# An encoder block on one core: the loads of the down projection issued as two halves each

## The chip, the cores and the metric

The kernel runs on one core of a Trainium2 chip. The metric is the device time of one execution in microseconds (us); the kernel before has a median of 2466.58 us over three runs.

## The reference, cut to what matters

The program is one encoder layer on 2048 tokens of width 1024: an mLSTM mixer, a squared-ReLU MLP, a gated embedding and a final norm. The change is in the second half of the MLP.

```python
def sqrelu_mlp(xn, w1, w2):              # w1: 1024 x 4096, w2: 4096 x 1024
    return jnp.square(jax.nn.relu(xn @ w1)) @ w2
...
    h = h + sqrelu_mlp(rmsnorm(h, norm_mlp[i]), mlp_w1[i], mlp_w2[i])
```

## The kernel before, in words

Every product is made of three fp32r matmuls: each operand is split into a rounded high part (ScalarE, a CAST) and a low part (VectorE, a subtraction), both 512 columns at a time. The two MLP products also use a seven-product block scheme: an operand's four blocks are combined by additions before the split, and seven products (tiles pa, pb, pc in PSUM) take the place of eight.

The MLP's up half writes the hidden activations to HBM (`hid_d`). The **down half** reads them back. It is a list of 48 jobs (`down_job`). A job handles 256 tokens (`q`, eight groups of them) and two or three "pairs" of w2's row tiles: 16 pairs in all enter a sliding set (`ENTER`), so each pair is used by eight jobs in a row. Most jobs have three pairs, the others two. A job's result is added to `h1_d` in HBM by two accumulating DMAs (`add_to`, on GpSimd's queue), each of 128 rows of 4 KB. For groups q of 0 to 3 the rows are one block of 128; for groups 4 to 7 they are addressed by `by_quad`, as 4 x 32 rows.

Three kinds of transfers matter:

- `Left2.dma` loads a job's activations (tiles `hst`), two jobs ahead (`run7`). With more than two pairs it makes two DMAs, one for each c, of 128 partitions x 3 x 256 floats, which is 3 KB in one piece per partition (line 937 of the kernel before). With two pairs it is one DMA of 2 KB pieces (line 942).
- `Right2.dma` loads a pair's two row tiles of w2 (`wst`), 4 KB in one piece per partition (line 954), about one job before they are used.
- `add_to` accumulates (line 1162), on GpSimd's queue; the loads are on SyncE's (SP).

SP works through its queue in order. A load waits there until the buffers of its tile (a pool of 39) are free, that is until TensorE, VectorE or ScalarE is done with the tile that was there; every DMA also uses one of eight completion counters (DMAHW0 to DMAHW7) in turn, and waits for the DMA eight issues earlier.

When a load lands, VectorE makes the sums (`sa` from `hst`, `ta` from `wst`) and low parts, ScalarE the high parts; both engines also evacuate PSUM (`e`, `o`), in one order, so that an evacuation behind a late load's sum waits with it. TensorE takes the operands (`op`) one job later. The first use of a pair of `hst` tiles is `s12`, which reads both; the first use of a pair of `wst` tiles is `t12`, which reads both halves of the first and then the second.

All of these are written through helpers, so that the profile gives most of them line 100; tiles tell them apart.

Of the kernel before, what the change touches and what calls it, by code (L numbers as in the profile page):

```python
# [16 lines left out]
P = 128  # L17
# [18 lines left out]
def hybrid_mlstm_kernel(  # L36
# [20 lines left out]
    x, p, out = x[0], p[0, 0], out[0]  # L57
    w_in, w_out, w1, w2, ple_w, gate_w = (w[0] for w in (w_in, w_out, w1, w2, ple_w, gate_w))
# [15 lines left out]
    def Ht(name, shape, dt=F32):  # L74

        return sb.tile(shape, dt, tag="H", bufs=NH, name=name)
# [32 lines left out]
    V, A, G, TE, SP = Engine(nc.vector), Engine(nc.scalar), nc.gpsimd, Engine(nc.tensor), nc.sync  # L109
# [80 lines left out]
    class Weight:  # L190
# [6 lines left out]
        def dma(self):  # L197
            self.st = Ht("wst", self.shape)
            at = 0
            for src in self.srcs:  # L200
                n = src.shape[-1]
                SP.dma_start(self.st[..., at:at + n], src)
                at += n
# [20 lines left out]
    def run(jobs):  # L224
        def dma(i):
            if i < len(jobs):
                for w in jobs[i].weights:
                    w.dma()
        for i, j in enumerate(jobs):
            if i == 0 and j.ready:  # L230
                dma(1)
            elif i == 0:
                dma(0)
                for w in j.weights:
                    w.prep()
                dma(1)
            dma(i + 2)
            nxt = [w.prep for w in jobs[i + 1].weights] if i + 1 < len(jobs) else []
            if any(j.at):
                for i, g in enumerate(j.groups):  # L240
                    for f in j.at[i] + (nxt if i == 0 else []) + [g]:
                        f()
            else:
                weave(j.groups, nxt + j.side)


    class Prep:
        order = staticmethod(lambda z: z.rearrange("p (j t) -> p j t", j=4))
        rows = staticmethod(lambda d, t: d[t])
# [102 lines left out]
    def by_quad(d, t):  # L352

        q = t % 4
        return d[t - q:t - q + 4, 32 * q:32 * q + 32]

    class Early(Prep):
        order = staticmethod(by_tile)
        rows = staticmethod(lambda d, t: by_quad(d, t))
# [474 lines left out]
    hid_d = dram.tile([NQ, P, 2, NF // 2, 256], F32, name="hid_d")  # L834
# [89 lines left out]
    class Left2(Left):  # L924
# [6 lines left out]
        def dma(self):  # L931
            n, p0 = self.n, self.p0
            if n > 2:
                self.r = []
                for c in range(2):
                    t = Ht("hst", [P, n, 256])
                    SP.dma_start(t, hid_d[self.q, :, c, p0:p0 + n])
                    self.r.append(t)
            else:
                t = Ht("hst", [P, 2, n, 256])  # L940
                self.r = [t[:, 0], t[:, 1]]
                SP.dma_start(t, hid_d[self.q, :, :, p0:p0 + n])

    class Right2:
# [5 lines left out]
        def dma(self):  # L950
            self.r = []
            for j in range(2):
                t = Ht("wst", [P, 2, 512])
                SP.dma_start(t, w2[(2 * self.p + j) * P:(2 * self.p + j + 1) * P, :].rearrange("p (l n) -> p l n", l=2))
                self.r.append(t)

        def preps(self):
# [46 lines left out]
    class Tokens0(Right1):  # L1004


        rows = staticmethod(lambda d, t: d[t])
# [60 lines left out]
    class Tokens1(Right1):  # L1068


        rows = staticmethod(by_quad)
# [233 lines left out]
    p0 = pa[1][0]  # L1305
# [127 lines left out]
    l = ch[NC - 1]  # L1433
# [31 lines left out]
    n = ENTER[-1] + NQ  # L1465
# [83 lines left out]
```

## Time and profile before

| | |
|---|---|
| runs (three) | median 2466.58 us, 2463.69 to 2473.59 |
| profiled execution | 2461.31 us, of which the span is 2459.6 us |
| TensorE's granted clock, mean | 0.998 of full speed (2.4 GHz) |
| TensorE busy | 2401.7 us, 98% of the span |
| down half, first job's operands to last job | about 1555 to 2215 us of the span |

The busy time of matmuls is modelled, so 98% says that TensorE hardly ever stood still, not that it ran at its peak. The span is that of the profiled execution; the runs around it are some 5 us longer at the median.

### The profile page before, as it was taken

The page shows a single profiled execution, that of the slowest core. Times are in us where ns is not written, and L with a number is a line of the kernel's source. Part 1 is how long each engine was busy: PE and PEld are TensorE (multiplying, and loading weights), DVE is VectorE, ACT ScalarE, POOL GpSimd, SP SyncE. Part 2 cuts the span into 40 slices and gives each one's busy share as a digit, 9 for nine tenths or more (in the row PEclk, how much of TensorE's full clock was granted, in tenths as well). Part 3 has the DMA queues.
Part 4 walks back from the last instruction along what each step waited for, and adds up shares of the span by engine and source line. Part 5 has one row for each costly group of instructions (what it writes and reads, how often), then busy time and mean ns, then how long its engine had stood idle before and what let it go on. Part 6 is the DMA issues. An engine that isn't in the chain of part 4 may idle for free.

```text
span 2459.6 us, 31654 instructions
## 1 busy us (share of the span) xinstructions
PE 2401.7 (98%) x11413; PEld 1977.9 (80%) x11413; DVE 1517.4 (62%) x2533; ACT 1132.5 (46%) x2134; POOL 592.2 (24%) x609
## 2 busy tenths in 40 slices
PE   8999999999999899999999999999999999999998
PEld 6988898788888787888888888787887888887776
DVE  5152436556778889566674555766676667666665
ACT  5031314436777775333353333444443444445554
POOL 1030022124433324335733333011111111110000
PEclk9999999999999999999999999999999999999999
DMA  8177337858667675455773332567677776893211
GB/s 258 45 202 248 92 95 241 279 197 313 229 226 257 224 244 173 129 170 162 262 233 113 103 107 70 163 141 183 142 180 170 172 171 156 184 222 103 78 55 49
DMA packets 270133, 420.72 MB, mean 171 GB/s; under 512 B 46440, under 2 KB 181992, under 8 KB 269976
## 3 DMA queue, kind: packets, MB, share of 16 engines
q1 hardware_dynamic: 211416, 299.03, 37.1%
q0 software_dynamic: 58272, 119.15, 20.8%
q8 instruction: 89, 1.46, 0.2%
q14 instruction: 68, 0.56, 0.1%
q10 hardware_dynamic: 288, 0.52, 0.1%
HBM read 253.43 MB, written 165.01 MB: 170 GB/s over the span
## 4 chain that ended last, share of the span: by engine, by line
PE 52%; DVE 4%; ACT 2%; DMA 2%; issue 1%; SPq 0%; POOL 0%; ACTq 0%; DVEq 0%; POOLq 0%
PE pa L100 27%; PE pb L100 13%; PE pc L100 7%; PE pg L100 4%; PE pl L100 1%; DVE h L100 1%; ACT L100 1%; DMA hst<-hid_d 1%; DVE xs L100 1%; PE pt L100 1%; DMA wst<-in_ple_w 1%; DMA wst<-in_mlp_w 1%; DVE op L100 1%; DVE rst L100 1%; ACT g L100 0%
## 5 line engine op out<-in xcount | busy, mean ns | idle before, releaser
L100 PE MATMUL pa<-op 128*128 128x512 f32 x3072 | 753.3, 394 | 7.2 <-ACT e L100 4.2
L100 PEld LDWEIGHTS pa<-op 128*128 128x128 f32 x3072 | 575.5, 188 | 146.2 <-ACT e L100 7.1
L100 PE MATMUL pb<-op 128*128 128x512 f32 x1536 | 384.0, 394 | 0.9 <-DVE op L100 0.8
L100 PEld LDWEIGHTS pb<-op 128*128 128x128 f32 x1536 | 288.1, 188 | 69.9 <-DVE op L100 1.1
L100 PE MATMUL psf<-xT,whi 128*128 128x512 f32 x1024 | 320.8, 394 | 0.0
L100 DVE TENSOR_TENSOR op<-sa,op 128x768 fp32r<-128x768 f32 (+2 forms) x160 | 167.5, 1053 | 138.7 <-ACT op L100 107.0
L1162 POOL DMA_DIRECT2D h_d<-o x96 | 93.1, 977 | 563.3 <-DVE o L100 515.0
L100 PEld LDWEIGHTS psf<-xT,whi 128*128 128x128 f32 x1024 | 191.3, 188 | 43.7
L100 ACT COPY e<-pa 128x512 f32<-128x512 f32 x160 | 93.7, 586 | 261.3 <-PE pa L100 260.5
L100 ACT CAST op<-sa 128x768 fp32r<-128x768 f32 (+2 forms) x160 | 139.6, 879 | 148.1 <-PE pb L100 69.0
L100 PE MATMUL psf<-xT,wlo 128*128 128x512 f32 x512 | 201.8, 394 | 0.0
L100 PE MATMUL pc<-op 128*128 128x512 f32 x768 | 191.6, 394 | 0.2 <-DVE op L100 0.2
L100 PEld LDWEIGHTS pc<-op 128*128 128x128 f32 x768 | 144.1, 188 | 34.3 <-DVE op L100 0.6
L100 PE MATMUL psv<-whi,xT 128*128 128x272 f32 (+2 forms) x720 | 160.9, 317 | 0.6 <-DVE xT L98 0.6
L100 DVE TENSOR_TENSOR op<-wst,op 128x512 fp32r<-128x512 f32 x96 | 108.5, 1132 | 29.7 <-ACT op L100 16.5
L100 PEld LDWEIGHTS psv<-whi,xT 128*128 128x128 f32 x720 | 118.6, 188 | 9.9 <-DVE xT L98 0.8
L884 POOL TENSOR_TENSOR sa<-wst 128x512 f32<-128x512 f32 x32 | 59.1, 1848 | 264.4 <-PE pb L100 159.2
L100 ACT CAST op<-wst 128x512 fp32r<-128x512 f32 x96 | 79.3, 834 | 92.8 <-DVE op L100 58.9
L100 PEld LDWEIGHTS psf<-xT,wlo 128*128 128x128 f32 x512 | 96.1, 188 | 22.4
L100 PE MATMUL psv<-wlo,xT 128*128 128x272 f32 (+2 forms) x360 | 114.0, 317 | 0.0
L100 DVE TENSOR_TENSOR wlo<-wst,whi 128x1024 fp32r<-128x1024 f32 (+2 forms) x64 | 77.0, 1212 | 59.4 <-ACT whi L100 50.3
L100 PE MATMUL pso<-whi,hThi 128*128 128x512 f32 x256 | 102.1, 400 | 3.2 <-ACT nt L100 1.9
(228 smaller groups left out, 4271.6 us busy)
## 6 DMA issues: line engine op xcount, KB each, us to landing
wst<-in_mlp_w SPq DMA_DIRECT2D x96, 512.0 KB
h_d<-o POOLq DMA_DIRECT2D x96, 512.0 KB, 12.4
hid_d<-e SPq DMA_DIRECT2D x128, 256.0 KB
hst<-hid_d SPq DMA_DIRECT2D x64, 384.0 KB
wst<-in_mlstm_w_in SPq DMA_DIRECT2D x44, 512.0 KB
vst<-v_d SPq DMA_DIRECT2D x31, 512.0 KB
raw<-in_x SPq DMA_DIRECT2D x16, 512.0 KB
kq<-kq_d SPq DMA_DIRECT2D x16, 512.0 KB
```

Of the source, the lines that this page charges most:

```text
L100: r = f(*a, **kw)
L884: eng.tensor_tensor(s[:, 0], r1[:, :, P:], r2[:, :, P:], op=add_)
L1162: G.dma_start(rows(h1_d, 2 * q + i), o[i], accum_op=add_)
```

## The change

Each of the 32 row tiles of w2 is loaded by two DMAs, one for each half of its columns (2 KB per partition). Each of the 64 `hst` tiles of jobs with more than two pairs is loaded by two DMAs along its pairs: with three pairs the first moves one pair (1 KB per partition) and the second two (2 KB). Jobs of two pairs load as before. There are 96 more DMAs; the bytes are the same.

```diff
                 for c in range(2):
                     t = Ht("hst", [P, n, 256])
-                    SP.dma_start(t, hid_d[self.q, :, c, p0:p0 + n])
+                    for a, b in ((0, n // 2), (n // 2, n)):
+                        SP.dma_start(t[:, a:b], hid_d[self.q, :, c, p0 + a:p0 + b])
                     self.r.append(t)
...
             for j in range(2):
                 t = Ht("wst", [P, 2, 512])
-                SP.dma_start(t, w2[(2 * self.p + j) * P:(2 * self.p + j + 1) * P, :].rearrange("p (l n) -> p l n", l=2))
+                rows = w2[(2 * self.p + j) * P:(2 * self.p + j + 1) * P, :].rearrange("p (l n) -> p l n", l=2)
+
+                for l in range(2):
+                    SP.dma_start(t[:, l], rows[:, l])
                 self.r.append(t)
```

On SP's queue, at the place of the loads that were issued from 1658 to 1673 us of the span: two activation loads of two-pair jobs, a pair of w2, and two jobs' activations, with what each waits for. Before:

```order
L942 DMA hst<-hid_d 128x2x512 [waits DMAHW3_49,DMAHW4_49,DVE_49,PE_49]
L942 DMA hst<-hid_d 128x2x512 [waits DVE_49,PE_49]
L954 DMA wst<-in_mlp_w 128x1024 [waits DMAHW5_49,DVE_49]
L954 DMA wst<-in_mlp_w 128x1024 [waits DMAHW6_49,DVE_49]
L937 DMA hst<-hid_d 128x768 [waits DMAHW7_49,PE_49]
L937 DMA hst<-hid_d 128x768 [waits DMAHW0_49,PE_49]
L937 DMA hst<-hid_d 128x768 [waits DMAHW1_49,PE_49]
L937 DMA hst<-hid_d 128x768 [waits DMAHW2_49,PE_49]
```

The same place with the change:

```order
L943 DMA hst<-hid_d 128x2x512 [waits DMAHW3_49,DVE_49,PE_49]
L943 DMA hst<-hid_d 128x2x512 [waits DMAHW4_49,DVE_49,PE_49]
L958 DMA wst<-in_mlp_w 128x512 [waits DMAHW5_49,DVE_49]
L958 DMA wst<-in_mlp_w 128x512 [waits DMAHW6_49]
L958 DMA wst<-in_mlp_w 128x512 [waits DMAHW7_49,DVE_49]
L958 DMA wst<-in_mlp_w 128x512 [waits DMAHW0_49]
L938 DMA hst<-hid_d 128x256 [waits DMAHW1_49,PE_49]
L938 DMA hst<-hid_d 128x512 [waits DMAHW2_49]
L938 DMA hst<-hid_d 128x256 [waits DMAHW3_49,PE_49]
L938 DMA hst<-hid_d 128x512 [waits DMAHW4_49]
L938 DMA hst<-hid_d 128x256 [waits DMAHW5_49,PE_49]
L938 DMA hst<-hid_d 128x512 [waits DMAHW6_49]
```

The first half of a tile waits for the tile's buffer as the whole did, the second half only for its counter; eight DMAs now span half as many bytes.

The instruction order is laid out by a scheduler, and with other DMAs it puts a few evacuations elsewhere. On VectorE, where that pair of w2 is prepared (1673 to 1680 us; `ta` and `op` from `wst`, `o` an evacuation):

```order
-L100 TENSOR_TENSOR ta<-wst 128x512
-L100 TENSOR_TENSOR o<-pb,e 128x512
-L100 TENSOR_TENSOR ta<-wst,ta 128x512
-L100 TENSOR_TENSOR op<-wst,op 128x512
-L100 TENSOR_TENSOR ta<-wst 128x512
+L100 TENSOR_TENSOR o<-pb,e 128x512
+L100 TENSOR_TENSOR ta<-wst 128x512 x2
+L100 TENSOR_TENSOR ta<-wst,ta 128x512
+L100 TENSOR_TENSOR op<-wst,op 128x512
```

One evacuation moved ahead of the sums that wait for w2. TensorE's order is the same in both kernels.

## Rows read from the trace of the kernel before

**Rows 1.** The page, part 1: busy time of each engine, share of the span, instructions; and TensorE's granted clock in 40 slices, in tenths.

```profile
PE 2401.7 (98%) x11413; PEld 1977.9 (80%) x11413; DVE 1517.4 (62%) x2533; ACT 1132.5 (46%) x2134; POOL 592.2 (24%) x609
...
PEclk9999999999999999999999999999999999999999
```

**Rows 2.** Busy time by stretch of the down half: stretch, its length, busy us of each engine, granted clock, busy share of the DMA engines, GB/s. The first row is nearly the whole stage.

```profile
1585.00:2130.00 545.00, 540.36 (x2326) 435.77 (x2325) 377.19 (x580) 246.19 (x382) 88.84 (x98) 1.00 0.72 167
...
1660.00:1700.00 40.00, 36.88 (x157) 28.83 (x156) 29.25 (x47) 20.78 (x34) 7.35 (x8) 1.00 0.81 193
1700.00:1740.00 40.00, 40.00 (x174) 32.40 (x173) 26.58 (x42) 18.32 (x29) 5.58 (x6) 1.00 0.71 166
...
1860.00:1900.00 40.00, 38.49 (x166) 30.90 (x165) 25.68 (x41) 16.12 (x24) 8.84 (x10) 1.00 0.72 171
```

**Rows 3.** Who TensorE waited for from 1555 to 2200 us: total us, times, longest.

```profile
PE pa L100 <- ACT e L100: 2.7, 2, 1.5
PE pa L100 <- DVE o L100: 1.9, 1, 1.9
PE pb L100 <- DVE op L100: 0.8, 1, 0.8
PE pc L100 <- DVE op L100: 0.2, 1, 0.2
```

**Rows 4.** Waits of VectorE and ScalarE for loads, from 1555 to 2200 us: total us, times, longest.

```profile
DVE sa L100 <- DMA hst<-hid_d: 15.0, 3, 7.0
ACT op L100 <- DMA hst<-hid_d: 10.9, 5, 4.0
DVE ta L100 <- DMA wst<-in_mlp_w: 4.5, 2, 2.8
ACT op L100 <- DMA wst<-in_mlp_w: 3.1, 1, 3.1
```

**Rows 5.** The chain of waits from 1660 to 1700 us, and then that from 1855 to 1880 us: start, us, what. A DMA's row runs from its issue to its landing.

```profile
1664.68 13.05 DMA wst<-in_mlp_w
...
1677.82 0.69 DVE ta L100
...
1848.72 19.07 DMA hst<-hid_d
...
1867.81 0.51 ACT op L100
1868.32 0.49 ACT e L100
```

**Rows 6.** The timeline of TensorE at the same two places: start, us, engine, operation, count, and in brackets the idle time before and what ended it.

```profile
1681.02 1.66 PE L100 MATMUL pa<-op 128*128 128x512 f32 x6 [1.15 <-ACT e L100]
...
1686.78 2.59 PE L100 MATMUL pa<-op 128*128 128x512 f32 x10 [1.86 <-DVE o L100]
...
1868.86 2.35 PE L100 MATMUL pa<-op 128*128 128x512 f32 x9 [1.51 <-ACT e L100]
```

**Rows 7.** What SP's loads cost to issue: ns min/median/max of one, first and last start.

```profile
L937 SPq DMA_DIRECT2D hst<-hid_d x64: 319/331/2047, 1582.9 to 2109.5; - x64
...
L954 SPq DMA_DIRECT2D wst<-in_mlp_w x32: 332/359/1731, 1555.2 to 2081.0; - x32
```

**Rows 8.** Who SP waited for from 1585 to 2130 us, its three longest.

```profile
SPq L937 <- PE pb L100: 120.5, 21, 16.2
SPq L954 <- PE pb L100: 100.1, 9, 13.0
SPq L937 <- PE pa L100: 55.3, 10, 17.8
```

**Rows 9.** SP's timeline in three short stretches: start, us, engine, line, count of loads. Stretches 1848 to 1855, 1855 to 1862 and 1879 to 1881 us.

```profile
1848.72 2.33 SPq L937 DMA_DIRECT2D hst<-hid_d  x2
...
1860.89 0.80 SPq L937 DMA_DIRECT2D hst<-hid_d  x2
...
1879.60 1.07 SPq L937 DMA_DIRECT2D hst<-hid_d  x2
```

**Rows 10.** DMA queues in short stretches: packets, MB, the time that they took as a share of 16 engines. First 1705 to 1711 us (6 us; two `hst` tiles, 256 packets of 3 KB and 32 of a few bytes), then 2064 to 2066.6 us (2.6 us; 256 of 2 KB and 16 small ones), then 1575.9 to 1577 us (1.1 us; 256 of 1 KB and 16 small ones).

```profile
q1 hardware_dynamic: 288, 0.79, 41.7%
q0 software_dynamic: 20, 0.04, 3.7%
...
q1 hardware_dynamic: 272, 0.52, 66.1%
...
q1 hardware_dynamic: 272, 0.26, 67.2%
```

**Rows 11.** The same view from 1936 to 1941 us (5 us), with the loads issued in it.

```profile
q1 hardware_dynamic: 407, 1.39, 86.3%
issues: line engine op xcount, KB each, median us to landing
wst<-in_mlp_w SPq DMA_DIRECT2D x2, 512.0 KB
hst<-hid_d SPq DMA_DIRECT2D x2, 384.0 KB
```

**Rows 12.** The same view from 1873 to 1874 us (1 us), and then from 1857 to 1859 us (2 us) with its count of packets by size; q0 is GpSimd's queue with the accumulates, q1 SP's with the loads.

```profile
q0 software_dynamic: 25, 0.10, 51.2%
...
DMA packets 86, 0.26 MB, mean 131 GB/s; under 512 B 0, under 2 KB 23, under 8 KB 86
...
q0 software_dynamic: 43, 0.18, 43.9%
q1 hardware_dynamic: 43, 0.08, 12.8%
```

**Rows 13.** The accumulates into `h1_d` from 1585 to 2200 us.

```profile
L1162 POOL DMA_DIRECT2D h_d<-o x94: 836/970/1507, 1587.3 to 2198.3; - x94
...
DMA to landing us min/median/max: 5.1/11.5/20.2
```

## The prediction

> **What bounds the kernel now.** The page's busy times come first: TensorE is busy 98% of the span, at a granted clock that stays at its upper level [rows 1]. So only time in which TensorE stands still can be won, and only more of it can be lost. The change touches the down half, so next the busy time by stretch: of 545 us of the stage TensorE works 540.4 [rows 2]. Most stretches of 40 us are full, as the one from 1700 us; two are not: 36.88 from 1660 us and 38.49 from 1860 us. The waits of TensorE name what is missing: 2.7 + 1.9 + 0.8 + 0.2 = 5.6 us in the whole stage [rows 3]. It waits for evacuations on ScalarE and VectorE (`e`, `o`), which is not the cause: the timeline puts three of these waits, 1.15, 1.86 and 1.51 us, at 1681, 1687 and 1869 us [rows 6], and the chain of waits leads there from a w2 load that took 13.05 us from issue to landing, and from an activation load that took 19.07 us [rows 5]. A sum waited for the load, and the evacuation stood behind it in its engine's order. In all, VectorE and ScalarE waited 15.0 + 10.9 + 4.5 + 3.1 = 33.5 us for loads, in 11 waits [rows 4], and TensorE lost 5.6 us: 0.17 us for each us of theirs. The rest is covered, because operands are prepared a job ahead.
>
> So the question is whether halved loads land earlier or later than whole ones, above all the late ones.
>
> **What the change costs, part by part.**
>
> *Issue.* 96 more DMAs at 0.33 us [rows 7] are 32 us of SP's time. SP waited 120.5 + 100.1 + 55.3 us in its three longest waits alone, for buffers that TensorE still reads [rows 8], so its time as such is hidden. What can count is that the last half of a tile is issued 0.33 us after the first, and the second tile of a pair 0.33 us later still: 0.66 us on the last landing. Against that, a first half of 1 KB packets already keeps an engine busy for 8 x 0.046 = 0.37 us (below), so the second half's issue lies beside its transfer. I take between nothing and 0.66 us per late load: 11 x 0.66 x 0.17 = 1.2 us at the most, and 0.3 us as the value, since the row of the transfer covers it nearly.
>
> *Bytes and packets.* With hardly another queue active, a 3 KB packet took 0.417 x 96 / 256 = 0.156 us of an engine (96 = 16 engines x 6 us, the small packets left out), a 2 KB packet 0.661 x 41.6 / 256 = 0.107 us, a 1 KB packet 0.672 x 17.6 / 256 = 0.046 us [rows 10]. A tile in halves is 0.046 + 0.107 = 0.153 us per partition against 0.156: nothing. For w2, 2 x 0.107 = 0.214 against 4/3 x 0.156 = 0.208: nothing.
>
> A row on fixed costs: from 1936 to 1941 us four loads were issued, and 1.39 MB moved in 5 us with the engines 86.3% busy [rows 11]; loads overlap, and no fixed time is paid in turn. The Trainium skill, "DMA: Bandwidth & Descriptors", § Rules for kernel authors, advises few large transfers, and its § Anatomy of one DMA gives 2.0 us per DMA beside the bytes; taken as time in a row, 96 more would be an estimated 192 us, which the row does not bear out, and if they stay hidden, nothing.
>
> *Turns on a shared engine.* This is where small packets cost. The accumulates for token groups 4 to 7 go to 4 x 32 rows, and there are two per job. From 1873 to 1874 us nothing else was moving, and they kept 51.2% of the 16 engines busy, which is eight: 25 packets of 4 KB, 0.512 x 16 / 25 = 0.33 us each [rows 12]. I read this as four engines for each accumulate, with 32 packets on each, 32 x 0.33 = 10.5 us; the median landing of 11.5 us fits [rows 13]. While they hold an engine, a load gets one turn per accumulate packet, whatever its size: from 1857 to 1859 us the two queues moved 43 packets each, 23 of SP's of 1 KB and 20 larger [rows 12]. With four engines on either kind, a turn of both queues took 4 x 2 / 23 = 0.35 us with a 1 KB packet and 4 x 2 / 20 = 0.40 us with a 3 KB one. A tile has 8 packets on each engine, so a held engine passes a 3 KB tile in 8 x 0.40 = 3.2 us, and its halves in 8 x 0.35 + 8 x 0.375 = 5.8 us (2 KB taken between the two): 2.6 us later. A w2 tile doubles its turns too and I take the same 2.6 us. The bounds: nothing where the load already outlasts the accumulate's 32 packets (the 13.05 and 19.07 us of [rows 5] look like that, being longer than 10.5), and 2 x 2.6 = 5.2 us for a pair.
> The Trainium skill, "DMA: Bandwidth & Descriptors", § Queues, rings and completion order, says that an engine takes its queues in turn, one packet each; the 43 and 43 agree. By that rule alone, with every late load in a held engine, the sum below would be twice as large.
>
> Value: the holding accumulates belong to 24 of 48 jobs, so half of the 11 late loads, 2.6 us each: 11 x 0.5 x 2.6 = 14.3 us of engine waits, x 0.17 = 2.4 us of TensorE. Upper bound: every load of the 24 jobs late by 5.2 us, 125 us, x 0.17 = 21 us.
>
> *Counters.* A DMA waits for the one eight issues before, now half as many bytes back. At the slowest load, issued at 1848.72 us and landed at 1867.79 [rows 5], the next four loads stand at 1850.67 (inside the pair), 1860.89 twice and then 1879.60 [rows 9]; the eighth half after it is the one at 1879.60, long after the landing. Nothing here. In a closer burst, of three pairs within 10 us, SP would hold the ninth half until the first lands; seven others are in flight then, so the engines stay fed.
>
> *Order.* The scheduler moves a few evacuations; at the first late place `o<-pb,e` comes ahead of the sums that wait for w2. It was not the evacuation that stopped TensorE there (that was `o` on pa, after them), so nothing; the most it could win is all of the stage's 5.6 us. Sums that read both halves wait for both; only `op` on the first half of w2 could start earlier, and it stands behind such a sum.
>
> **Sum.** 0.3 + 2.4 = 2.7 us of TensorE waits more, on the profiled execution's 2461.3 us; the median of the runs stands 5.3 us above that, at 2466.6, so 2469.3 us. A measurement of this kernel can tell about 0.5%, 12.3 us, from no change, so this is none.
>
> **The rivals.**
> *All hidden, or the late loads gain.* If halves let sums start early or the moved evacuations stop waiting, at most the 5.6 us of [rows 3] go: 2461 us. For it: late loads are what stops TensorE. Against: the first sums read both tiles, and the last byte comes no earlier. For a gain of 12.3 us there isn't enough idle time in the stage.
> *Held engines make loads late in every job of groups 4 to 7.* The upper bound of the turns, 21 us: 2488 us, slower by 0.85%. It decides against my forecast once the 24 jobs lose over 12.3 / 24 = 0.5 us of TensorE each. For it: 19.07 us for one load shows how little margin some jobs have. Against: only 11 waits for loads in 48 jobs now, and a load cannot last longer than the accumulates plus its own bytes.
> *A gain elsewhere:* the rest of the program keeps its order on TensorE and its DMAs, so none.
>
> **How the numbers follow.** Chances: my forecast, a few us more with the waits at the same two or three places, 0.62; hidden or a small gain (2461 to 2467), 0.26; held engines throughout, 0.12, of which two thirds reach past 0.5%. The range holds the first two and the lower part of the third: from 2459 us (all 5.6 us gone, and 2 us of spread between runs) to 2481. Slower by over 0.5%: 0.08. Faster by over 0.5%: 0.02, for which I have no mechanism. Within: 0.90.
>
> **What would show it.** TensorE's waits in the stage should come to some 8 us in place of 5.6, at the same kinds of evacuation. VectorE's and ScalarE's waits for `hst` and `wst` should rise from 33.5 to about 48 us. Stretches with a held engine should still show equal counts of packets on both queues, with more of SP's under 2 KB, and the accumulates should land no later. The prediction is wrong if TensorE's busy time in the down half falls below 0.97 of it with new waits in the jobs of groups 4 to 7, or if loads land clearly earlier and the 5.6 us are gone.

## The result, and the profile after

| | before | changed |
|---|---|---|
| median of 12 runs each | 2465.85 us | 2477.14 us |
| ratio | | 1.0038, 95% interval 1.0025 to 1.0050 |
| profiled execution, span | 2459.6 us | 2474.5 us |

The halved loads make the kernel slower by 0.38%, 9 to 11 us: inside the bound of 0.5% and inside the range, with the sign that was forecast, but about four times the 2.7 us of the sum.

Of the 14.9 us between the two spans, 3.4 lie ahead of the down half. This is read from a wait that both traces have at the same matmul, near the stage's start: at 1578.05 us before, at 1581.46 us after. Up to there the programs differ only in the stage's first loads, and other profiled executions differ by 1 to 8 us at this place (below). What is left, 14.9 - 3.4 = 11.5 us, is put down to the down half. The same working serves for all runs below. It takes in what follows the stage, which differs from the kernel before by up to 1.1 us: from the same wait to the end of the stage's last matmul the two traces have 630.4 and 642.5 us, 12.1 us more. Where this matters, the second figure is given too, as *stage alone*.

Busy time by stretch of the changed kernel, as in [rows 2] (the columns as there; first nearly the whole stage):

```profile
1585.00:2130.00 545.00, 533.90 (x2285) 429.96 (x2284) 372.08 (x576) 243.68 (x378) 87.22 (x96) 0.99 0.72 165
1660.00:1700.00 40.00, 36.49 (x156) 28.70 (x155) 29.55 (x48) 19.93 (x32) 6.03 (x6) 1.00 0.80 190
1860.00:1900.00 40.00, 37.23 (x155) 29.76 (x154) 24.94 (x38) 15.01 (x22) 6.72 (x9) 0.96 0.64 142
1900.00:1940.00 40.00, 35.59 (x148) 28.43 (x147) 20.13 (x31) 13.91 (x22) 5.57 (x6) 0.96 0.68 154
2100.00:2140.00 40.00, 38.08 (x163) 30.19 (x162) 27.99 (x43) 19.25 (x31) 6.47 (x6) 1.00 0.80 161
```

TensorE works 533.9 us of 545 where it worked 540.4. The stretches that lacked time before lack a little more, and two new ones do, from 1900 and from 2100 us. Two stretches show a mean granted clock of 0.96. TensorE's timeline shows each place (start, us of the group, count, the idle time before it and what ended it):

```profile
1581.46 0.73 PE L100 MATMUL pc<-op 128*128 128x512 f32 x2 [0.18 <-DVE op L100]
...
1684.94 1.67 PE L100 MATMUL pa<-op 128*128 128x512 f32 x6 [1.64 <-ACT e L100]
1690.40 2.58 PE L100 MATMUL pa<-op 128*128 128x512 f32 x10 [1.87 <-DVE o L100]
...
1873.73 3.77 PE L100 MATMUL pa<-op 128*128 128x512 f32 x9 [2.77 <-ACT e L100]
1917.40 5.99 PE L100 MATMUL pa<-op 128*128 128x512 f32 x18 [4.41 <-DVE o L100]
...
2036.39 4.46 PE L100 MATMUL pa<-op 128*128 128x512 f32 x18 [0.40 <-DVE o L100]
...
2135.98 2.34 PE L100 MATMUL pa<-op 128*128 128x512 f32 x9 [0.98 <-ACT e L100]
2139.26 2.34 PE L100 MATMUL pb<-op 128*128 128x512 f32 x9 [0.94 <-ACT e L100]
```

Waits of VectorE and ScalarE for loads, and the waits of TensorE, 1555 to 2215 us (total us, times, longest), as in [rows 3, 4]:

```profile
ACT op L100 <- DMA hst<-hid_d: 26.9, 9, 7.2
DVE sa L100 <- DMA hst<-hid_d: 15.1, 6, 6.2
DVE ta L100 <- DMA wst<-in_mlp_w: 11.9, 4, 5.8
ACT op L100 <- DMA wst<-in_mlp_w: 2.7, 1, 2.7
...
PE pa L100 <- DVE o L100: 6.7, 3, 4.4
PE pa L100 <- ACT e L100: 5.4, 3, 2.8
PE pb L100 <- ACT e L100: 0.9, 1, 0.9
PE pb L100 <- DVE op L100: 0.8, 1, 0.8
PE pc L100 <- DVE op L100: 0.2, 1, 0.2
```

The waits for loads went from 33.5 to 26.9 + 15.1 + 11.9 + 2.7 = 56.6 us, 20 in place of 11. TensorE's went from 5.6 to 14.0 us: 8.4 us more. Most of the rest is in the matmuls that follow the two longest waits: nine took 3.77 us behind 2.77 us of waiting, eighteen 5.99 us behind 4.41. Nine run in 2.35 us behind a wait of 1.51 [rows 6], and eighteen in 4.46 us in the row at 2036 us, so some 1.4 and 1.5 us are lost, 2.9 in all. (The last 0.8 us of the 12.1 is in idle time around the same places, too short for the list of waits.) The granted clock goes with these matmuls; stretches behind the first of these waits, with TensorE's busy time and clock:

```profile
1874.00:1878.00 4.00, 4.00 (x12) 0.64 0.72 163
1878.00:1882.00 4.00, 4.00 (x19) 1.00 0.52 124
```

The clock's mean is 0.64 there, part of the stretch at the lower level (1.2 of 2.4 GHz), and 1.00 four microseconds later.

The chain of waits leads to a load at each place, as in [rows 5]: from 1855 us, from 1895 us, and from 2100 us (twice).

```profile
1858.53 14.07 DMA hst<-hid_d
...
1901.72 13.63 DMA wst<-in_mlp_w
...
2110.34 14.66 DMA hst<-hid_d
...
2126.57 11.22 DMA hst<-hid_d
```

The place at 1917 us is the new one that costs most: the last half of a pair of w2, issued at 1901.72 us, landed after 13.63 us. VectorE's sum waited for it, the evacuations `o<-pa,e` and `o<-pb,e` stood behind the sum, and TensorE behind them.

This load was not only long under way, it was also issued late. SP's timeline has the pair's two whole tiles before, and then the four halves; below them are SP's issues of `hst` and w2 in the whole changed kernel (ns min/median/max, as in [rows 7]):

```profile
1890.73 1.82 SPq L954 DMA_DIRECT2D wst<-in_mlp_w  x2
...
1897.04 6.20 SPq L958 DMA_DIRECT2D wst<-in_mlp_w  x4
...
L938 SPq DMA_DIRECT2D hst<-hid_d x128: 319/466/5394, 1587.4 to 2126.6; - x128
...
L958 SPq DMA_DIRECT2D wst<-in_mlp_w x64: 328/423/2548, 1558.6 to 2095.4; - x64
```

Of the 192 issues 48 took more than 1 us, up to 5.4; before it was 12 of 96, up to 2.0. The last of the four halves was issued 4.7 us after the first; before, the second tile was issued 0.4 us after the first. TensorE's wait at this place is 4.41 us.

### The profile page after: what moved, and what is told of

It reads as the page before. It is cut to its first block, busy times and chain, and to the rows that moved or that the text cites. A ratio compares the mean times of both kernels' runs of the same rounds, so it can differ in the third digit from the quotient of the medians.

```text
span 2474.5 us, 31828 instructions
## 1 busy us (share of the span) xinstructions
PE 2408.6 (97%) x11413; PEld 1982.2 (80%) x11413; DVE 1520.0 (61%) x2533; ACT 1133.1 (46%) x2134; POOL 591.1 (24%) x609
## 4 chain that ended last, share of the span: by engine, by line
PE 83%; DVE 7%; DMA 4%; ACT 4%; issue 2%; SPq 0%; POOL 0%; DVEq 0%; ACTq 0%; POOLq 0%
PE pa L100 26%; PE psf L100 14%; PE pb L100 13%; PE psv L100 7%; PE pc L100 6%; PE pso L100 5%; PE pg L100 5%; DMA hst<-hid_d 2%; PE pn L100 2%; PE pu L100 1%; PE pl L100 1%; PE pt L100 1%; DVE rst L100 1%; DMA wst<-in_mlp_w 1%; DVE xs L100 1%
## 5 line engine op out<-in xcount | busy, mean ns | idle before, releaser
L100 PEld LDWEIGHTS pa<-op 128*128 128x128 f32 x3072 | 577.5, 189 | 155.7 <-ACT e L100 10.5
## 6 DMA issues: line engine op xcount, KB each, us to landing
h_d<-o POOLq DMA_DIRECT2D x96, 512.0 KB, 12.2
```

What stands on the lines that cost most here:

```text
L100: r = f(*a, **kw)
```

## The experiments

The theory, as in the prediction: the accumulates for groups 4 to 7 hold four engines each, and a load there gets one packet per accumulate packet, so that more and smaller packets land later (*turns*). The rivals: the 96 DMAs as such, by SP's issue and the eight counters; and the evacuations that the scheduler moved. Times in the down half are those of the profiled executions, worked out as above, each less those of the kernel before. The kernel before, once more, tells what that is worth:

> The kernel before, once more, to see how far one profiled execution differs from another: TensorE's waits in the down half again 5 to 6 us at the same three places, VectorE's and ScalarE's waits for loads 30 to 37 us; differences ahead of the down half of some us, which then are no matter of the change.

```diff
(no change)
```

Its span is 2459.7 us; TensorE waited 2.2 + 1.9 + 0.8 + 0.2 = 5.1 us in the stage, at the same places, and the engines 9.8 + 8.5 + 4.3 + 2.9 = 25.5 us for loads. So the waits for loads differ by some 8 us between executions of one program (30 to 37 us were expected), the time in the down half by less than 1 us. The changed kernel, once more:

> The changed kernel, once more: +7 to +12 us, TensorE's waits in the down half again some 14 us at the same places (1685 to 1690, 1873, 1917, 2136 us), and a lower granted clock for the matmuls that follow the waits of more than 2 us.

```diff
(the change as it is)
```

Ratio 1.0050 (1.0034 to 1.0065). The first wait is at 1580.21 us in a span of 2473.2: 13.6 - 2.2 = 11.4 us in the down half, as the first time. TensorE's waits come to 12.2 us, but not all at the same places: its timeline has 0.87 us near 1912 us here, and 4.31 near 2033 us, where eighteen matmuls then took 7.18 us.

```profile
1912.07 4.44 PE L100 MATMUL pa<-op 128*128 128x512 f32 x18 [0.87 <-DVE o L100]
...
2033.44 7.18 PE L100 MATMUL pa<-op 128*128 128x512 f32 x18 [4.31 <-DVE o L100]
```

**One part of the change alone.**

> Only the activation tiles are loaded in halves; w2 as before. If the loads lose turns to the accumulates (theory of the turns), this keeps the hst part of the loss: the late places at 1873 and 2136 us of the changed kernel were hst loads, the one at 1917 us a w2 load, so about half of the +9.4 us: +3 to +7 us, with TensorE waits of 7 to 11 us in the down half. If SP's issue and its eight counters are the cause, the loss goes by the number of added DMAs, 64 of 96: +6 us. If the moved evacuations are the cause, all of it stays, since the order of VectorE and ScalarE is that of the changed kernel: +9 us.

```diff
-                    SP.dma_start(t, hid_d[self.q, :, c, p0:p0 + n])
+                    for a, b in ((0, n // 2), (n // 2, n)):
+                        SP.dma_start(t[:, a:b], hid_d[self.q, :, c, p0 + a:p0 + b])
```

Ratio 1.0016 (1.0004 to 1.0028). In the down half 10.0 - 7.2 = 2.8 us (stage alone 3.5), the lower end of the theory's 3 to 7. It carries the changed kernel's order of VectorE and ScalarE, and loses less than half as much: the moved evacuations are not what costs 9 us. By the number of DMAs, two thirds of the loss were due. The two waits near 2136 us are here (1.13 and 1.90 us); the one near 1873 us has not grown (1.35 us), so it was not due to the halves of `hst`.

> Only w2's row tiles are loaded in halves; the order of VectorE and ScalarE is that of before. Theory of the turns: the w2 part of the loss, +2 to +6 us, with the w2 load issued at about 1900 us landing some 2.6 us later than before. Issue and counters: 32 of 96 DMAs, +3 us. Moved evacuations: nothing, within 1 us.

The edit, against the changed kernel (w2's halves stay):

```diff
-                    for a, b in ((0, n // 2), (n // 2, n)):
-                        SP.dma_start(t[:, a:b], hid_d[self.q, :, c, p0 + a:p0 + b])
+                    SP.dma_start(t, hid_d[self.q, :, c, p0:p0 + n])
```

Ratio 1.0032 (1.0021 to 1.0043), with a third of the DMAs and the order of before: in the down half 8.6 - 2.5 = 6.1 us (stage alone 5.0). The wait near 1873 us is here, with 2.78 us, and that near 1917 us has 0.93; the 4.41 us of the changed kernel took both kinds of halves. The waits for loads in this run, 1555 to 2225 us:

```profile
ACT op L100 <- DMA hst<-hid_d: 24.0, 7, 6.3
DVE sa L100 <- DMA hst<-hid_d: 21.6, 5, 8.3
DVE ta L100 <- DMA wst<-in_mlp_w: 13.2, 6, 4.4
```

Not only w2 is later (4.5 to 13.2 us on VectorE), but also the whole `hst` loads, 25.9 to 45.6 us in all. I read this as their standing behind w2's halves in the same queue: counted from the stage's first wait, the load behind the wait at 1873 us was issued 1.4 us later than before.

**As many DMAs, but no smaller packets.**

> The kernel before with one more DMA of 64 bytes (one packet, into a tile that nothing reads) behind each of the 64 hst and 32 w2 loads: as many DMAs on SP's queue and counters as in the changed kernel, packets of the loads as before, order of the engines in the down half as before. Theory of the turns: within 2 us of the kernel before. Issue and counters: +5 to +9 us, with TensorE waits of 10 us or more in the down half.

```diff
                     SP.dma_start(t, hid_d[self.q, :, c, p0:p0 + n])
+                    SP.dma_start(sb.tile([1, 16], F32, tag="dmy", bufs=8, name="dmy"), w2[0:1, 0:16])
...
+                SP.dma_start(sb.tile([1, 16], F32, tag="dmy", bufs=8, name="dmy"), w2[0:1, 0:16])
```

Ratio 1.0002 (0.9989 to 1.0014). But the run does not do what it was meant to do. SP's rows of the two added lines (ns min/median/max, first and last start) show all 96 small DMAs at the program's start, from 23 to 108 us:

```profile
L938 SPq DMA_DIRECT2D dmy<-in_mlp_w x64: 222/250/323, 26.8 to 107.5; - x64
...
L956 SPq DMA_DIRECT2D dmy<-in_mlp_w x32: 222/252/882, 23.2 to 102.8; - x32
```

They do not stand behind the loads, so the down half is that of the kernel before, and the run says nothing about added issues and counters there. It is one more measure of the spread: waits for loads 9.8 + 8.4 + 4.5 + 3.1 = 25.8 us, and 1.1 us more in the down half (stage alone 1.8, of which 1.6 is in nine matmuls that took 3.92 us behind a wait of 1.76). With the first two traces of the kernel before, the stage alone runs from 629.6 to 632.2 us, so differences of 2 to 3 us between single traces are not much more than their spread.

> The same tiles are loaded by two DMAs each, but halved by partitions (64 and 64): as many DMAs as in the changed kernel, packets of 3 KB and 4 KB as before. Theory of the turns: no more turns, so the loss goes: within 3 us of the kernel before, landings of the late loads as before (13 us at the w2 place near 1665 us, no 4 us wait of TensorE near 1917 us). Issue and counters: as slow as the changed kernel, +9 us. The scheduler's order differs from both kernels here, which can add or take some us at single places.

Again against the changed kernel:

```diff
-                    for a, b in ((0, n // 2), (n // 2, n)):
-                        SP.dma_start(t[:, a:b], hid_d[self.q, :, c, p0 + a:p0 + b])
+                    for a in (0, 64):
+                        SP.dma_start(t[a:a + 64], hid_d[self.q, a:a + 64, c, p0:p0 + n])
...
-                for l in range(2):
-                    SP.dma_start(t[:, l], rows[:, l])
+                for a in (0, 64):
+                    SP.dma_start(t[a:a + 64], rows[a:a + 64])
```

Ratio 1.0042 (1.0029 to 1.0055): as slow as the changed kernel, against the theory's forecast and as the rival of issue and counters had it. But the order of VectorE and ScalarE differs much here, and TensorE's in the first jobs, and the trace shows another kind of loss. In the first jobs of the stage, from 1582 to 1591 us, TensorE waits for operands with no load in the chain, and its matmuls come some 7 us later behind it, which is the most of what it loses; the waits at 1681 and 1687 us are gone; and one of 4.96 us at 1883 us is due to an `hst` tile that was issued only at 1873.99 us. TensorE's timeline in this run, and SP's issue just ahead of that tile's:

```profile
1585.01 0.73 PE L100 MATMUL pc<-op 128*128 128x512 f32 x2 [0.79 <-DVE op L100]
...
1590.29 1.22 PE L100 MATMUL pa<-op 128*128 128x512 f32 x2 [1.47 <-DVE op L100]
...
1883.27 3.91 PE L100 MATMUL pa<-op 128*128 128x512 f32 x9 [4.96 <-ACT e L100]
...
L938 SPq DMA_DIRECT2D hst<-hid_d x1: 12742/12742/12742, 1861.2 to 1861.2; - x1
```

The tile was issued late because the issue before it took 12.74 us, beside accumulates of 4 x 32 rows. So this wait of 4.96 us came with packets of 3 KB, without more turns: a long issue is a second way in which held engines make loads late. Of the 42.0 us of waits for `hst` (24.0 and 18.0) the rest is not explained. For w2 the theory holds: 5.7 us of waits (5.0 of them on one ScalarE evacuation) where the changed kernel has 14.6.

**Smaller packets, but no more DMAs.**

> The number of DMAs and the order of every engine are those of the kernel before; only the hst tiles of three pairs are laid out with gaps, so that a partition's 3 KB arrive as three pieces of 1 KB. Theory of the turns: 24 turns per engine and tile in place of 8, 24 x 0.35 = 8.4 us on a held engine where it took 3.2, twice the delay of the changed kernel's hst tiles: +6 to +20 us, with VectorE's and ScalarE's waits for hst above 42 us. Issue and counters, or moved evacuations: nothing, within 2 us, waits for hst near 26 us.

```diff
-                    t = Ht("hst", [P, n, 256])
+                    t = Ht("hst", [P, n, 320])[:, :, :256]
```

Ratio 1.0018 (1.0007 to 1.0029), in the down half 6.7 - 4.5 = 2.2 us (stage alone 2.9), with every engine's order as before. The waits for `hst` are 24.9 + 15.3 = 40.2 us, in place of 25.9 and, the second time, 18.3. Turns are at work: from 1862 to 1864 us the accumulates moved 46 packets and SP's queue 50, all of 1 KB (DMA queues in this run: packets, MB, share of 16 engines):

```profile
q0 software_dynamic: 46, 0.19, 47.0%
q1 hardware_dynamic: 50, 0.05, 9.2%
```

That agrees with the Trainium skill, "DMA: Bandwidth & Descriptors", § Queues, rings and completion order, on engines that take their queues in turn. That section's packet is a bundle, typically of 9 to 17 descriptors; here it is single records of 1 and 4 KB that keep step, 50 and 46 in 2 us, in which an engine passes some six of the 4 KB at 0.33 us each. But 24 turns cost no more than the 16 of the `hst` halves alone (2.8 us, stage alone 3.5), where I had expected 6 to 20 us: the number of turns does not go straight into the time.

**Without held engines.**

> The loads are whole, as before; each accumulate of 4 x 32 rows (groups 4 to 7) is issued as four DMAs of 32 rows, so that it is spread over all engines, 2 packets each, and none holds four of them with 32. Theory of the turns: the long landings go (19.07 us at 1849 us, 13.05 at 1665), VectorE's and ScalarE's waits for hst and wst fall from 33.5 to below 15 us, TensorE's waits in the down half from 5.6 to some 2 us: 0 to 5 us faster than before. If the lateness is SP's (issue, buffers, counters) and not the accumulates': no change in these waits.

```diff
-            G.dma_start(rows(h1_d, 2 * q + i), o[i], accum_op=add_)
+            d = rows(h1_d, 2 * q + i)
+            if q < 4:
+                G.dma_start(d, o[i], accum_op=add_)
+            else:
+                for j in range(4):
+                    G.dma_start(d[j].rearrange("t (l n) -> t l n", l=2), o[i][32 * j:32 * j + 32], accum_op=add_)
```

Ratio 0.9958 (0.9944 to 0.9972): 2456.4 us, the fastest kernel of this study, 0.4% faster than the kernel before. In the down half -5.2 - 1.4 = -6.6 us (stage alone -6.0); TensorE's waits account for 5.6 - 1.0 = 4.6 of it. Set side by side, the matmuls of the two traces show all of the 6.0 us at the places where TensorE waited before: 3.9 us near 1681 and 1687, 1.8 near 1869, and 0.3 near 2123, where the idle time was too short for the list. Its waits from 1555 to 2225 us (the one for a load of this stage, then all of TensorE's):

```profile
DVE sa L100 <- DMA hst<-hid_d: 1.1, 1, 1.1
PE pb L100 <- DVE op L100: 0.8, 1, 0.8
PE pc L100 <- DVE op L100: 0.2, 1, 0.2
```

The accumulates into `h1_d`, from issue to landing, from 1585 to 2215 us:

```profile
DMA to landing us min/median/max: 2.9/6.1/11.0
```

All late loads but one of 1.1 us are gone. The medians of 6.1 us here and 11.5 in [rows 13] mix both kinds of accumulates. In the kernel before, the eight of one run through groups 4 to 7 (issued from 1847 to 1895 us) landed as in the first row below, the eight of groups 0 to 3 ahead of them as in the second; in the changed kernel those of groups 4 to 7 (1851 to 1901 us) as in the third.

```profile
DMA to landing us min/median/max: 13.8/16.2/18.1
...
DMA to landing us min/median/max: 5.4/8.1/10.1
...
DMA to landing us min/median/max: 14.7/16.2/18.5
```

So the accumulates of 4 x 32 rows take some 16 us to land, whether the loads are halved or not, and in four parts each part lands after 6.0 us at the median. From a job's first issue to its last landing it was 17.8 us at the median for groups 4 to 7, and is 10.4. (Spreading also takes the packets under 512 bytes from 21524 to 6175 between 1585 and 2215 us; whether that matters is not tested.) By stretch, TensorE works the whole 545 us of the stage:

```profile
1585.00:2130.00 545.00, 545.00 (x2352) 441.44 (x2352) 379.61 (x584) 247.50 (x385) 172.12 (x218) 1.00 0.75 170
```

> The changed kernel (all tiles in halves) with the same spread accumulates. Theory of the turns: halving costs next to nothing without held engines: within 2 us of the run with whole loads and spread accumulates, 7 us or more faster than the changed kernel, w2 waits of VectorE near 5 us in place of 11.9. Issue and counters: it stays 6 to 9 us slower than whole loads with spread accumulates.

```diff
(the change, and the accumulates as in the run before this one)
```

Ratio 0.9981 (0.9970 to 0.9992), 2461.9 us. TensorE's waits in the stage are the same 0.8 and 0.2 us, and the one wait for a load that grew (from the same view) is hidden. And 2 of the 192 issues of w2 and `hst` take more than 1 us, where it was 48:

```profile
DVE sa L100 <- DMA hst<-hid_d: 5.6, 2, 3.0
...
L958 SPq DMA_DIRECT2D wst<-in_mlp_w x64: 327/422/972, 1562.0 to 2083.1; - x64
...
L938 SPq DMA_DIRECT2D hst<-hid_d x128: 319/422/3782, 1590.7 to 2111.7; - x128
```

The first wait stands at 1584.86 us in a span of 2460.7: 1.1 - 6.8 = -5.7 us in the down half, against -6.6. The 0.9 us between them lies behind the stage. The stage's last matmuls, first with whole loads (first wait at 1579.46 us) and then with halves:

```profile
2202.28 1.55 PE L100 MATMUL pa<-op 128*128 128x512 f32 x6
...
2207.76 1.55 PE L100 MATMUL pa<-op 128*128 128x512 f32 x6
```

That is 624.4 us from the wait to the end of the last matmul with whole loads and 624.5 with halves: halving costs 0.1 us of the stage here, and 12.1 with held engines. All 96 added DMAs are in this kernel, so their number alone, with its issues and counters, is not what costs 9 us: as a cause apart from the held engines this rival falls. The medians differ by 5.5 us, though, so both ran once more:

> Spread accumulates and whole loads, once more, beside the same with halved loads on the same chip. The first profiles of the two agree in the down half to 0.1 us, while their medians are 5.5 us apart; in the profiles that lies ahead of the down half, where the two programs have the same instructions. If it is chance of single executions: 2456 to 2461 us, within 3 us of the halved one.

> Spread accumulates and halved loads, once more. If the 5.5 us were chance: within 3 us of the whole loads, with the same waits of TensorE in the down half, 1.0 us. If halving costs something without held engines that one profile did not show: again 4 to 7 us slower than whole loads, with waits in the down half.

```diff
(the two kernels before this, unchanged)
```

2458.3 us, ratio 0.9969 (0.9960 to 0.9978), and 2460.6 us, 0.9976 (0.9966 to 0.9986). With halves one issue took 6.8 us here, but again only 2 of 192 more than 1 us. In the down half -6.6 and -5.9 us, and 624.4 and 624.5 us from the first wait to the end of the last matmul once more. In the second pair the whole loads were later ahead of the stage (the same first wait at 1585.73 us, with halves at 1582.21), in the first pair it was the other way (1579.46 and 1584.86): that part is chance of single executions. By the medians whole loads are the faster both times, by 5.5 and 2.3 us. The traces don't put this into the stage, and what it is stays open.

## Why the prediction was right, and where it was off

The time lies inside the range, and the loss came as forecast, from loads that are late beside held engines. That it counts as no change is in part luck: the second ratio, 1.0050, is the bound of 0.5% itself, and the sum had 2.7 us, a fifth of the bound.

- **What bounds the kernel: right.** 8.4 of the stage's 12.1 us are TensorE waiting for evacuations that stand behind sums that wait for loads. That was [rows 3 to 6], with more places. TensorE's waits came to 14.0 us, and 12.2 the second time, where some 8 were forecast; it still worked 0.98 of the stage.
- **Issue, 0.3 us: wrong beside held engines.** The prediction let SP take 0.33 us for each issue, at most 0.66 us on a late landing, beside its transfer. In the changed kernel 48 of 192 issues took more than 1 us, up to 5.4 (39 and up to 7.8 the second time), and at the costliest place the last half was issued 4.7 us after the first. The 2.0 us in [rows 7] and the 2.33 us for two issues in [rows 9] were the signs of it. The ratio of 1.0002 with 96 small DMAs doesn't speak against it, since none of them was in the down half. With spread accumulates it is 2 of 192, and the halves cost 0.1 us of the stage, so it goes with the held engines; why an issue takes longer beside them, no run shows. (The 2.0 us per DMA that the prediction sets beside this is, in the Trainium skill, "DMA: Bandwidth & Descriptors", § Anatomy of one DMA, a figure for DMAs issued by GpSimd; the loads here are SP's.)
- **Counters, nothing: right as far as it shows.** In the stage SP waited 6.0 us for earlier loads before, and 6.6 + 1.3 = 7.9 us with the change.
- **Bytes: right.** In the changed kernel the share of the DMA engines in the stage stayed at 0.72, as in [rows 2].
- **Turns on held engines, 2.4 us: the held engines were right, the size was not, and turns are one of two ways.** That the held engines turn the change from nothing into a loss is shown by the two pairs with spread accumulates. That it is the turns is shown less well: equal counts of packets, and few waits for w2 when its packets stay whole, speak for them; 24 turns that cost no more than 16, and late `hst` loads with packets of 3 KB, do not. How the loss divides between turns and issue stays open. Two factors of the term were off. The waits for loads rose by 23.1 us (33.5 to 56.6) and the second time by 14.6 (to 48.1), where the sum had 14.3. And the 0.17 us of TensorE for each us of waiting, taken as a mean over the waits of before, was 8.4 / 23.1 = 0.36 for the added ones. I read this as waits that were just covered and are covered no more, so that the next us goes through in full; no run tests it. I had named a w2 pair as a place where the load already outlasted the accumulate; there (1685 and 1690 us) the waits indeed grew by just 0.5 us. The loss is at another w2 pair and at the `hst` loads near 1873 and 2136 us.
- **A reading that was wrong: how long the accumulates take.** The prediction worked out 10.5 us for the packets of an accumulate of groups 4 to 7, and took the median landing of 11.5 us for a sign of it. That median mixes two kinds: those accumulates land after some 16 us, those of groups 0 to 3 after some 8.
- **Not in the sum: w2's halves delay the `hst` loads that follow in the queue.** I had costed each load by its own turns. With w2 alone in halves `hst` waited 20 us more than in the first run of the kernel before, and 27 more than in the second.
- **Not in the sum: the clock.** 2.9 us of matmuls at the lower level behind the two longest waits. Before, the longest wait was 1.86 us, and nothing was lost behind it.
- **Order, nothing: right as far as it shows.** The wait behind `o` at the first place is 1.87 us, as it was 1.86 [rows 6], and the kernel with this order and whole w2 loads loses 2.8 us.
- **The rivals.** Neither all hidden nor a loss in every job; the accumulates of groups 4 to 7 landed no later, as forecast.

## What to carry to other kernels

Look at what else holds the DMA engines where a load is late: here it was a transfer whose outermost dimension is 4, some 16 us from issue to landing, and spreading it gave 8 to 10 us by the medians, 6.0 of them in this stage, which is all that TensorE lost there to late loads. On an engine that two queues share, the two moved equal counts of packets here (43 and 43, 46 and 50), so the one with smaller packets falls back, and issues of loads became long; don't cut a load into smaller pieces there unless something can start on the first. Price a delay at a place that already waits at its full size: a mean over hidden and bare waits is too kind. And find in the trace where an added instruction has ended up: the 96 small DMAs were to stand behind the loads, and all of them were issued in the first 108 us.

## What was not expected of the hardware

- A wait of TensorE can cost more than itself: behind waits of 2.77 and 4.41 us the granted clock fell, and 27 matmuls took 2.9 us longer. In the run with small DMAs nine matmuls took 3.92 us behind a wait of only 1.76, while ten after 1.87 us here lost nothing, so the length of the wait alone doesn't decide.
- An issue on SP's queue, 0.33 us at the median before, took up to 7.8 us in the two executions of the changed kernel and 12.74 with tiles halved by partitions. More than 1 us took 12 of 96 before, 48 and 39 of 192 with the change, and 2 of 192 with the accumulates spread as well.
- A 4 KB packet of an accumulate takes 0.33 us of an engine, twice a plain load's 3 KB (0.156) in [rows 10, 12]. The Trainium skill, "DMA: Bandwidth & Descriptors", § Why a DMA increments its semaphore by 16 and not by 1, has the number of engines follow from the outermost dimensions; 4 x 32 rows on four engines, and 32 rows per DMA on all, fit the two landings, some 16 us and 6.0 us.
